# A hybrid decoder layer on one core: the first weight units, the bias rows, the block turns and the key raws in another order

## The chip, the core and the metric

The kernel runs on one core of a Trainium2 chip. The metric is the device time of one execution in microseconds (us), as the median of several runs. The profile is of one execution: its "span" runs from the first to the last instruction of the program, and the execution's own time is a little longer than its span.

## What is computed

One layer for 256 tokens of width 2048, all in float32: a half-step SwiGLU block, a mixer (8 attention heads of 128 beside a state-space model, joined by one output projection), and a second half-step SwiGLU block.

```python
x = x + 0.5 * swiglu(rms_norm(x, ffn1_norm), gate, up, down)     # 2048 -> 5632 -> 2048
h = rms_norm(x, mix_norm) @ w_in                                 # q | k | v | u, 1024 columns each
attn = mixture_of_dilations(rms_norm(q), rms_norm(k), v, rel_bias)
y = gelu(s5_ssm(u, ...)); y = y * sigmoid(y @ glu_w + glu_b)
x = x + concat(attn, y) @ w_out
x = x + 0.5 * swiglu(rms_norm(x, ffn2_norm), gate2, up2, down2)
```

The three attention patterns share one bias table (32 buckets by 8 heads). The kernel computes them as one softmax, for which `bias_rows` holds, for each distance, the one-hot bucket, a mask and the logarithm of how many patterns see it.

## The kernel before

**Units.** Every large product is a list of passes (`Pass`): 256 tokens (two PSUM accumulators of 128) by 512 output columns, over all blocks of 128 of the contraction. A pass is cut into groups of four such blocks, and a group into two units. A unit is two blocks by two token halves by three matmuls of 128x128 by 128x512: float32 is split into a high and a low float32r part, and high x high (line 336), high x low weight (337) and low activation x high weight (338) are summed. So a unit is 12 matmuls. The first feed-forward block is 264 units, the mixer 104, the second feed-forward block 264.

**One loop, `run`, sets the order** on all engines. A group's weights (1 MB) are loaded on SyncE's (SP's) queue into one of three buffers `raw`; `split` makes of each half the high part `wh` on ScalarE (ACT, line 292) and the low part `wl` on VectorE (DVE, lines 295 and 297), four units ahead at most (`WB`). After each unit's matmuls `step` advances every other piece of work, written as Python generators: one `yield` is one unit of TensorE (PE) time. Since each engine runs its instructions strictly in the order written, these counts fix who stands behind whom. The very first pass pair (gate and up columns 0 of the first block) is the only one whose groups are interleaved; everything later goes pass after pass.

**The start.** x arrives in pieces of 256 and 512 columns; `Normed.feed` turns them with PE transposes (line 194), and `close` makes `xth` and `xtl`, their high and low parts with the gain. Normalising by the row's root mean square comes later, at eviction (`rstd`, finished by small GpSimd (POOL) operations).

**Bias table.** After the first squares, `other_gains` loads small gains on POOL's queue, and four steps later turns them on PE. `bias_table` then loads the bucket table (`rel`) and `bias_rows` (`oh`) on the same queue, and two steps later a PE matmul (line 1146) joins them. Between the two, `ssm_prepare` has begun: it loads its parameters on POOL's queue, turns b on PE (line 500), and for four pieces of 16 groups forms powers on DVE (676 to 678), which PE multiplies (708).

**Turns by blocks.** `by_blocks` transposes 32x32 blocks on DVE into one tile `blocks` (139), stores it to DRAM (142) and reads it back with rows and blocks exchanged (145), so that PE has no part in it. Each feed-forward column group uses it for its hidden values (in `up_done`); so do the residual's blocks 0 to 2 when they feed the next stage (`feed_by_blocks`). Residual block 3, which is ready last, is turned by PE (`feed`). Column groups 5 and later wait for the state-space preparation, whose space they reuse.

**Mixer.** Passes come in the order u0, u1, k0, q0, k1, q1, v0, v1. The tile `qk` has two halves. `qk_done` writes the raw projection of a pass to the first half, q's turned copy goes to the second. `k_prepare` takes squares on ACT, an inverse root on DVE (lines 113 to 121), scales on ACT (894) and turns on PE (880); `q_scale` turns its scales on PE (906); `head` scores four heads of each half (926 to 956). Beside them DVE runs the state-space scan, step after step (795 to 797).

Of the kernel before, what the change touches and what calls it, by code (L numbers as in the profile page):

```python
# [16 lines left out]
P = 128  # L17
# [21 lines left out]
class Pass:  # L39
    def __init__(self, w, n, stat, ks, done=None, delay=0, pre=None, box=None, opens=True, bank="acc"):  # L40
        self.w, self.n, self.stat, self.ks, self.done = w, n, stat, list(ks), done
        self.delay, self.pre, self.opens, self.bank = delay, pre, opens, bank
        self.box = {} if box is None else box


@with_exitstack
def hybrid_layer_kernel(
# [209 lines left out]
    def run(passes, extra, start):  # L257
        g, u = passes[:2]
        groups = [(g, 0), (u, 0), (g, 4), (u, 4), (g, 8), (g, 12), (u, 8), (u, 12)]
        for p in passes[2:]:  # L260
            for k0 in p.ks:
                groups.append((p, k0))
# [4 lines left out]

        def dma():
# [3 lines left out]
            src = p.w[k0 * P:(k0 + 4) * P, p.n * 512:(p.n + 1) * 512].rearrange("(k p) n -> p k n", p=P)  # L272
            if i == 0:
                for k in range(2):
                    sync.dma_start(out=r[:, k:k + 1], in_=src[:, k:k + 1])
                extra(0)
                sync.dma_start(out=r[:, 2:4], in_=src[:, 2:4])
            else:
                sync.dma_start(out=r, in_=src)
            raws[i] = r  # L280
            st["dma"] += 1
            extra(i + 1)

        def split():
            u = st["split"]
            i, s = divmod(u, 2)
# [16 lines left out]
        def ahead(u):  # L303
            while st["dma"] < ng and st["dma"] < st["split"] // 2 + RAWB:
                dma()
            if st["split"] == 0:
                start()
            while st["split"] < 2 * ng and st["split"] <= (u + WB - 1 if u else 0):
                split()
                if st["split"] == 1:  # L310
                    start()
                while st["dma"] < ng and st["dma"] < st["split"] // 2 + RAWB:
                    dma()

        for i, (p, k0) in enumerate(groups):
            if k0 == p.ks[0]:
# [6 lines left out]
            for s in range(2):  # L323
                u = 2 * i + s
                ahead(u)
                h, l = wts.pop(u)
                order = [(kk, t) for kk in range(2) for t in range(NT)]
                if s == 1 and k0 == p.ks[-1]:
                    order = [(kk, t) for t in range(NT) for kk in range(2)]
                for kk, t in order:  # L330
                    k = k0 + 2 * s + kk
                    sh, sl = p.stat(k)
                    first = p.opens and k == p.ks[0]
                    last = p.done is not None and k == p.ks[-1] + 3
                    c = slice(t * P, (t + 1) * P)
                    pe.matmul(acc[t], sh[:, c], h[:, kk, :], start=first, stop=False)  # L336
                    pe.matmul(acc[t], sh[:, c], l[:, kk, :], start=False, stop=False)  # L337
                    pe.matmul(acc[t], sl[:, c], h[:, kk, :], start=False, stop=last)  # L338
                if s == 1 and k0 == p.ks[-1] and p.done:
                    spawn(call(p.done, acc), p.delay)  # L340
                step()


    def ffn(norm, w_gate, w_up, w_down, done, first):
# [31 lines left out]
        def up_done(c):  # L376
            def f(acc):
# [31 lines left out]
    def residual(norm, factor):  # L409
        def done(n):  # L410
            def f(acc):
# [3 lines left out]
                spawn(norm.feed(n) if n == 3 else norm.feed_by_blocks(n))  # L415
# [12 lines left out]
    def ssm_prepare():  # L428
# [237 lines left out]
        for pc in range(4):  # L666
# [218 lines left out]
    def k_prepare(raw, dst):  # L885
# [9 lines left out]
        yield 2  # L895
        yield from flipped(raw, dst, ident, 1.0)

    def q_scale(n, raw):
# [5 lines left out]
        yield 2  # L904
# [5 lines left out]
    def q_flip(n, raw, dst):  # L910
        while mx["scored"] < 4 * n:
            yield
        yield from flipped(raw, dst, flip, qkg)

    def head(h):
# [3 lines left out]
        qt = mx["qk"][:, 1024:2048].rearrange("p (h s) -> p h s", h=4)[:, i, :]  # L919
# [67 lines left out]
    def mixer(norm, out_done):  # L987
# [20 lines left out]
        def qk_done(which, n):  # L1008
            def f(acc):
                assert not any(alive(mx[x]) for x in ("prep_k0", "prep_k1", "rq0", "qT0") if x in mx)  # L1010
                raw = mx["qk"][:, 0:1024].rearrange("p (t x) -> p t x", t=NT)
# [4 lines left out]
                else:  # L1016
                    dst = mx["qk"][:, 1024:2048].rearrange("p (h s) -> p h s", h=4)
# [58 lines left out]
        for n in range(2):  # L1076
            ps.append(Pass(w_in[0], 6 + n, norm.stat, ks, u_done(n)))
# [18 lines left out]
    with tc.manual_schedule():  # L1096
# [18 lines left out]
        def other_gains():  # L1115
# [3 lines left out]
            pool.dma_start(out=grow[49:50], in_=k_norm)  # L1119
            pool.memset(flip, 0.0)  # L1120
# [13 lines left out]
            yield  # L1134
            yield from bias_table()

        def bias_table():
            rel = small([34, NH], "rel")
            pool.memset(rel, 1.0)
            pool.dma_start(out=rel[0:32], in_=rel_bias)  # L1140
            oh = slots.tile([34, SPAN], F32, name="oh", tag="s1a")
            pool.dma_start(out=oh, in_=bias_rows)
            yield
            yield
# [106 lines left out]
```

## Time and profile before

| | us |
|---|---|
| median of 3 runs | 1803.52 |
| lowest, highest run | 1800.95, 1804.94 |
| profiled execution, its own time | 1803.12 |
| its span | 1801.2 |
| PE busy | 1786.6 (99%) |
| DVE busy | 1058.7 (59%) |
| ACT busy | 845.0 (47%) |

Times in the profile are counted from the span's start. A row of the timeline gives start, duration, engine, line, operation, what it writes and reads, and in brackets how long the engine was idle ahead of it and what ended that. Matmuls overlap, so a matmul of 0.39 us is followed by the next about 0.23 us later; PE's busy share says that something was under way, not that it ran at full rate. The granted clock is the share of full speed that PE was given.

### The profile page before, as it was taken

The numbers are of one execution on the slowest core, as the hardware profiler recorded it, in microseconds if no ns is written. First come the engines' busy times: TensorE is split into PE (matmuls) and PEld (weight loads), VectorE is DVE, ScalarE is ACT, GpSimd is POOL, SyncE is SP. The second block draws the span as 40 slices with busy tenths as digits, with TensorE's granted clock in tenths as the row PEclk, the third lists the DMA queues.
The fourth block names the chain that finished last, engine by engine and source line by source line (L and its number), as shares of the span: only waits on it lengthen the run. The fifth ranks groups of instructions, "written<-read, shape, count | busy, mean of one in ns | idle before, by whom it ended". The sixth has DMA issues, their size and how long they took to land.

```text
span 1801.2 us, 21490 instructions
## 1 busy us (share of the span) xinstructions
PE 1786.6 (99%) x8399; PEld 1475.0 (82%) x8399; DVE 1058.7 (59%) x1368; ACT 845.0 (47%) x1087; POOL 79.3 (4%) x151
## 2 busy tenths in 40 slices
PE   9999999999999999999999999999999999999998
PEld 7788888788888888888788888888888888888887
DVE  5688888455555455544985665555555555544443
ACT  5454444444444444447666555444444444443332
POOL 0400222100000000010000001000000000000000
PEclk9999999999999999999999999999999999999999
DMA  7867988877766676598576585777777677766652
GB/s 257 236 209 228 290 287 281 249 234 220 218 218 206 205 221 221 195 315 284 158 261 203 187 255 190 218 223 212 212 223 219 210 214 222 222 208 210 210 198 105
DMA packets 211013, 402.21 MB, mean 223 GB/s; under 512 B 9581, under 2 KB 40902, under 8 KB 209249
## 3 DMA queue, kind: packets, MB, share of 16 engines
q1 hardware_dynamic: 202672, 378.57, 65.9%
q0 software_dynamic: 6416, 19.13, 3.7%
q10 hardware_dynamic: 1824, 3.15, 0.6%
q8 instruction: 65, 1.06, 0.2%
q14 instruction: 36, 0.29, 0.0%
HBM read 370.00 MB, written 33.44 MB: 224 GB/s over the span
## 4 chain that ended last, share of the span: by engine, by line
PE 93%; DVE 4%; DMA 1%; POOL 1%; ACT 1%; issue 1%; SPq 0%; POOLq 0%; DVEq 0%; ACTq 0%
PE acc L336 30%; PE acc L338 30%; PE acc L337 30%; DVE wl L297 1%; DVE s1a L795 1%; DMA oh<-in_bias_rows_dram 0%; DVE s1a L796 0%; PE tp L336 0%; PE tp L338 0%; PE tp L337 0%; DMA h_d<-blocks 0%; ACT wh L292 0%; DVE slot L797 0%; PE tp L194 0%; PE tp L1108 0%
## 5 line engine op out<-in xcount | busy, mean ns | idle before, releaser
L297 DVE TENSOR_TENSOR wl<-raw,wh 128x1024 fp32r<-128x1024 f32 x628 | 768.6, 1226 | 682.3 <-ACT wh L292 681.9
L292 ACT ACTIVATE wh<-raw 128x1024 fp32r<-128x1024 f32 (+1 forms) x636 | 672.2, 1058 | 882.6 <-PE acc L338 859.3
L336 PE MATMUL acc<-wh,xth 128*128 128x512 f32 x1664 | 655.0, 394 | 1.4 <-ACT wh L292 1.4
L337 PE MATMUL acc<-wl,xth 128*128 128x512 f32 x1664 | 649.1, 390 | 2.7 <-DVE wl L297 2.2
L338 PE MATMUL acc<-wh,xtl 128*128 128x512 f32 x1664 | 649.2, 390 | 0.0
L337 PEld LDWEIGHTS acc<-wl,xth 128*128 128x128 f32 x1664 | 313.4, 188 | 67.5 <-DVE wl L297 2.7
L336 PEld LDWEIGHTS acc<-wh,xth 128*128 128x128 f32 x1664 | 313.2, 188 | 67.0 <-ACT wh L292 1.7
L338 PEld LDWEIGHTS acc<-wh,xtl 128*128 128x128 f32 x1664 | 313.0, 188 | 65.7
L336 PE MATMUL acc<-wh,hid 128*128 128x512 f32 x704 | 273.9, 389 | 0.0
L337 PE MATMUL acc<-wl,hid 128*128 128x512 f32 x704 | 273.9, 389 | 0.0
L338 PE MATMUL acc<-wh,hid 128*128 128x512 f32 x704 | 273.9, 389 | 0.0
L338 PEld LDWEIGHTS acc<-wh,hid 128*128 128x128 f32 x704 | 132.1, 188 | 27.5
L337 PEld LDWEIGHTS acc<-wl,hid 128*128 128x128 f32 x704 | 132.1, 188 | 27.5
L336 PEld LDWEIGHTS acc<-wh,hid 128*128 128x128 f32 x704 | 132.1, 188 | 27.4
L123 POOL TENSOR_TENSOR rs_t<-rstd 128x2 f32<-128x2 f32 x9 | 5.7, 630 | 637.9 <-DVE rstd L115 637.5
L139 DVE STREAM_TRANSPOSE blocks<-sil 128x512 f32<-128x512 f32 x44 | 28.6, 687 | 7.6 <-DMA h_d<-blocks 7.6
L424 POOL DMA_DIRECT2D out_dram<-res x6 | 3.3, 552 | 645.2 <-DVE res L422 645.1
L380 DVE SCALAR_TENSOR_TENSOR sil<-acc,rstd,sil 128x512 f32<-128x512 f32 x44 | 30.7, 740 | 0.0
L130 DVE TENSOR_TENSOR hid<-sil,hid 128x512 fp32r<-128x512 f32 x44 | 28.3, 684 | 0.0
L369 ACT ACTIVATE sil<-acc,rstd 128x512 f32<-128x512 f32 x44 | 27.5, 675 | 0.0
L129 ACT ACTIVATE hid<-sil 128x512 fp32r<-128x512 f32 x44 | 25.0, 614 | 0.0
L657 POOL DMA_DIRECT2D t_d<-k_d x32 | 18.0, 580 | 24.5 <-DMA k_d<-slot 24.2
(324 smaller groups left out, 848.7 us busy)
## 6 DMA issues: line engine op xcount, KB each, us to landing
raw<-in_ffn_w_up_dram SPq DMA_DIRECT2D x88, 1024.0 KB, 5.9
raw<-in_ffn_w_down_dram SPq DMA_DIRECT2D x88, 1024.0 KB, 5.1
raw<-in_ffn_w_gate_dram SPq DMA_DIRECT2D x87, 1024.0 KB, 5.8
raw<-in_w_in_dram SPq DMA_DIRECT2D x32, 1024.0 KB, 5.6
raw<-in_w_out_dram SPq DMA_DIRECT2D x16, 1024.0 KB, 6.0
h_d<-blocks SPq DMA_DIRECT2D x28, 512.0 KB, 7.0
sil<-h_d SPq DMA_DIRECT2D x88, 128.0 KB, 7.1
m_d<-s4b POOLq DMA_DIRECT2D x16, 256.0 KB, 4.9
```

The source lines that it names most:

```text
L129: act.activation(out=h, in_=src, func=AF.Copy)
L130: vec.tensor_tensor(out=l, in0=src, in1=h.bitcast(F32), op=ALU.subtract)
L139: vec.transpose(out=b[:, :, t].rearrange("p j (k c) -> p j k c", k=4), in_=src[:, t, :].rearrange("p (k j c) -> p j k c", k=4, j=4))
L292: act.activation(out=h[:, c], in_=src[:, c], func=AF.Copy)
L297: vec.tensor_tensor(out=l, in0=src, in1=h.bitcast(F32), op=ALU.subtract)
L336: pe.matmul(acc[t], sh[:, c], h[:, kk, :], start=first, stop=False)
L337: pe.matmul(acc[t], sh[:, c], l[:, kk, :], start=False, stop=False)
L338: pe.matmul(acc[t], sl[:, c], h[:, kk, :], start=False, stop=last)
L369: act.activation(out=sil[c][:, t, :], in_=acc[t], func=AF.Silu, scale=norm.scale(t))
L380: vec.scalar_tensor_tensor(out=a[:, t, :], in0=acc[t], scalar=norm.scale(t), in1=a[:, t, :], op0=ALU.mult, op1=ALU.mult)
L657: pool.dma_start(out=stores[0][1], in_=stores[0][2])
L795: vec.tensor_tensor(out=tm, in0=a8, in1=prev.unsqueeze(1).broadcast_to([P, 2, 2, NG]), op=ALU.mult)
```

## The change

Five edits, all of order; the arithmetic stays the same but for where a transpose is made.

1. **First units.** The first two groups (gate and up) are loaded in halves, and their units run as gate first half, up first half, gate second half, up second half. In the first unit the four high x high matmuls come first, then the low activations, then the low weights.
2. **Shared first passes.** A pass may be marked `shared`: it and the next are then interleaved as the first two of the program always were. u0 with u1 and the second feed-forward block's gate with up column 0 are marked too.
3. **Bias rows.** `rel` and `oh` are loaded right after the small gains, ahead of the state-space parameters, and their matmul comes one step earlier.
4. **Turns.** Residual block 3 is turned by `feed_by_blocks` like the others. A hidden turn waits until the one of the column group before has ended. The preparation has one step fewer per piece (behind its last powers).
5. **Keys.** k0 and q1 keep their raw projection in the second half of `qk`, and q's copy goes to the other half; scaled keys and q's inverse roots are used one step later (`yield 3`), and `q_flip` waits for its key to be prepared, no longer for four scored heads.

```diff
+        self.shared = shared
...
-        g, u = passes[:2]
-        groups = [(g, 0), (u, 0), (g, 4), (u, 4), (g, 8), (g, 12), (u, 8), (u, 12)]
-        for p in passes[2:]:
-            for k0 in p.ks:
-                groups.append((p, k0))
+        groups = []
+        passes = list(passes)
+        while passes:
+            p = passes.pop(0)
+            if p.shared:
+                q = passes.pop(0)
+                groups += [(p, 0), (q, 0), (p, 4), (q, 4), (p, 8), (p, 12), (q, 8), (q, 12)]
+            else:
+                groups += [(p, k0) for k0 in p.ks]
...
+        units = [(0, 0), (1, 0), (0, 1), (1, 1)] + [(i, s) for i in range(2, ng) for s in range(2)]
...
+            if i == 0:
+                rs = [rawp.tile([P, 4, 512], F32, name=nm("raw"), tag="raw") for _ in range(2)]
+                for v, a, b in ((0, 0, 1), (0, 1, 2), (1, 0, 2), (0, 2, 4), (1, 2, 4)):
+                    sync.dma_start(out=rs[v][:, a:b], in_=part(*groups[v])[:, a:b])
+                    if v == 1 and a == 0:
+                        extra(0)
...
+            order = [(kk, t, v) for kk in range(2) for t in range(NT) for v in range(3)]
+            if u == 0:
+                order = [(kk, t, v) for v in (0, 2, 1) for kk in range(2) for t in range(NT)]
...
-                    while c >= 5 and first and alive(mx["pre"]):
+                    while (c >= 5 and first and alive(mx["pre"])) or (c and alive(turn[c - 1])):
                         yield
...
-                           (lambda: finish(mx["pre"])) if c == 7 and first else None))
+                           (lambda: finish(mx["pre"])) if c == 7 and first else None, shared=c == 0))
...
-                spawn(norm.feed(n) if n == 3 else norm.feed_by_blocks(n))
+                spawn(norm.feed_by_blocks(n))
...
             for k in range(1, 9, 2):
                 powers(wk[:, :, k:k + 2, :], k, 2, cs, csw)
                 yield from beat()
-                if k != 3:
+                if k in (1, 5):
                     yield from beat()
...
-        yield 2
+        yield 3
         yield from flipped(raw, dst, ident, 1.0)
...
         rsqrt_(rs, ss, 8, 1.0 / HD)
-        yield 2
+        yield 3
         ps = tps()
         pe.matmul(ps[:, 0:8], flip, rs, start=True, stop=True)
...
-        while mx["scored"] < 4 * n:
+        while alive(mx[f"prep_k{n}"]):
             yield
...
-                raw = mx["qk"][:, 0:1024].rearrange("p (t x) -> p t x", t=NT)
+                o = 1024 if (which == "k") == (n == 0) else 0
+                raw = mx["qk"][:, o:o + 1024].rearrange("p (t x) -> p t x", t=NT)
...
-            ps.append(Pass(w_in[0], 6 + n, norm.stat, ks, u_done(n)))
+            ps.append(Pass(w_in[0], 6 + n, norm.stat, ks, u_done(n), shared=n == 0))
...
             pool.dma_start(out=grow[48:49], in_=q_norm)
             pool.dma_start(out=grow[49:50], in_=k_norm)
+            rel = small([34, NH], "rel")
+            pool.memset(rel, 1.0)
+            pool.dma_start(out=rel[0:32], in_=rel_bias)
+            oh = slots.tile([34, SPAN], F32, name="oh", tag="s1a")
+            pool.dma_start(out=oh, in_=bias_rows)
             pool.memset(flip, 0.0)
...
-            yield
-            yield from bias_table()
...
+            yield 2
             ps = tps()
             pe.matmul(ps[:NH, 0:SPAN], rel, oh, start=True, stop=True)
```

How the edits move instructions at three places, as the built programs list them (line, operation, what it writes and reads, shape; line numbers of the change's rows are the changed file's).

SP's queue at the start of the program: `res` is x, `raw_144` the gate's first group, `raw` of `up_dram` the up's. Before:

```order
L1100 DMA res_83<-in_x_dram 128x2x256
L275 DMA raw_144<-in_ffn_w_gate_dram 128x512 x2
L1184 DMA res_83<-in_x_dram 128x2x256
L277 DMA raw_144<-in_ffn_w_gate_dram 128x2x512
L279 DMA raw_149<-in_ffn_w_up_dram 128x4x512
L1187 DMA res_84<-in_x_dram 128x2x512
```

And now:

```order
L1117 DMA res_83<-in_x_dram 128x2x256
L288 DMA raw_144<-in_ffn_w_gate_dram 128x512 x2
L288 DMA raw_145<-in_ffn_w_up_dram 128x2x512
L1196 DMA res_83<-in_x_dram 128x2x256
L288 DMA raw_144<-in_ffn_w_gate_dram 128x2x512
L288 DMA raw_145<-in_ffn_w_up_dram 128x2x512
L1199 DMA res_84<-in_x_dram 128x2x512
```

The up's first half has come ahead of x's second 256 columns; the bytes up to x's next piece are the same.

DVE behind the state-space preparation, where the hidden turns of column groups 5 and 6 (`sil` to `blocks`) follow among the low weights. Before:

```order
L297 TENSOR_TENSOR wl_2838<-raw_2744,wh_2837 128x1024
L380 SCALAR_TENSOR_TENSOR sil_555<-acc_2684,rstd_137,sil_555 128x512
L380 SCALAR_TENSOR_TENSOR sil_555<-acc_2685,rstd_137,sil_555 128x512
L139 STREAM_TRANSPOSE blocks_2862<-sil_555 128x4x128 x2
L297 TENSOR_TENSOR wl_2868<-raw_2744,wh_2867 128x1024
L139 STREAM_TRANSPOSE blocks_2887<-sil_555 128x4x128 x2
L297 TENSOR_TENSOR wl_2891<-raw_2785,wh_2890 128x1024
```

And now, from the turn of group 5 up to that of group 6:

```order
L140 STREAM_TRANSPOSE blocks_2845<-sil_561 128x4x128 x2
L314 TENSOR_TENSOR wl_2849<-raw_2754,wh_2848 128x1024
L314 TENSOR_TENSOR wl_2868<-raw_2754,wh_2867 128x1024
L314 TENSOR_TENSOR wl_2886<-raw_2792,wh_2885 128x1024
L396 SCALAR_TENSOR_TENSOR sil_561<-acc_2710,rstd_137,sil_561 128x512
L396 SCALAR_TENSOR_TENSOR sil_561<-acc_2711,rstd_137,sil_561 128x512
L314 TENSOR_TENSOR wl_2908<-raw_2792,wh_2907 128x1024
L314 TENSOR_TENSOR wl_2926<-raw_2830,wh_2925 128x1024
L314 TENSOR_TENSOR wl_2942<-raw_2830,wh_2941 128x1024
L314 TENSOR_TENSOR wl_2960<-raw_2871,wh_2959 128x1024
L314 TENSOR_TENSOR wl_2976<-raw_2871,wh_2975 128x1024
L314 TENSOR_TENSOR wl_2994<-raw_2911,wh_2993 128x1024
```

One low weight stood between the two turns; now nine stand there (the last fence ends with the ninth), and group 6's turn follows those.

DVE in the mixer, where the inverse root of k1 (`qk_rs`) begins. Before, from the row behind the scan to that root's first rows:

```order
L947 RECIPROCAL stat<-stat 128x2
L948 SCALAR_TENSOR_TENSOR stat<-stat 128x2
L949 SCALAR_TENSOR_TENSOR stat<-stat 128x2
L113 TENSOR_SCALAR rs_ms_1018_6791<-qk_ss_6717 128x8
L114 TENSOR_SCALAR rs_i_6793<-rs_ms_1018_6791 128x8
L115 TENSOR_SCALAR qk_rs_6718<-rs_i_6793 128x8
```

And now:

```order
L963 RECIPROCAL stat<-stat 128x2
L964 SCALAR_TENSOR_TENSOR stat<-stat 128x2
L965 SCALAR_TENSOR_TENSOR stat<-stat 128x2
L950 SCALAR_TENSOR_TENSOR s5a_5910<-tp_6746,rq,s5b_5911 128x128
L952 SCALAR_TENSOR_TENSOR s5a_5910<-tp_6746,rq,s5b_5911 128x256
L956 TENSOR_REDUCE stat<-s5a_5910 128x1
L957 TENSOR_REDUCE stat<-s5a_5910 128x1
L958 TENSOR_SCALAR stat<-stat 128x2
L114 TENSOR_SCALAR rs_ms_1017_6787<-qk_ss_6706 128x8
```

The heads have slid one unit back, so that the fourth head's logits now stand in the same unit as k1's inverse root, ahead of it; the root itself has kept its unit, and PE's turn of k1 comes one unit later.

More of the change, by code (lines that the diff above doesn't have):

```diff
@@ L39, with __init__ @@
 class Pass:
-    def __init__(self, w, n, stat, ks, done=None, delay=0, pre=None, box=None, opens=True, bank="acc"):
+    def __init__(self, w, n, stat, ks, done=None, delay=0, pre=None, box=None, opens=True, bank="acc", shared=False):
         self.w, self.n, self.stat, self.ks, self.done = w, n, stat, list(ks), done
@@ L266, in run, with part, spent @@
         st = {"dma": 0, "split": 0}
+        units = [(0, 0), (1, 0), (0, 1), (1, 1)] + [(i, s) for i in range(2, ng) for s in range(2)]
+        def part(p, k0):
+            return p.w[k0 * P:(k0 + 4) * P, p.n * 512:(p.n + 1) * 512].rearrange("(k p) n -> p k n", p=P)
+        def spent():
+            n = st["split"]
+            return n // 2 if n >= 4 else max(0, n - 2)
         def dma():
@@ L270, in dma @@
             p, k0 = groups[i]
-            r = rawp.tile([P, 4, 512], F32, name=nm("raw"), tag="raw")
[L272 to L279, printed above, removed]
+            if i == 0:
[4 more added lines that the diff above has]
+                        extra(0)
+                raws[0], raws[1] = rs
+                st["dma"] = 2
+                extra(2)
+                return
+            r = rawp.tile([P, 4, 512], F32, name=nm("raw"), tag="raw")
+            sync.dma_start(out=r, in_=part(p, k0))
             raws[i] = r
@@ L303, in ahead @@
         def ahead(u):
-            while st["dma"] < ng and st["dma"] < st["split"] // 2 + RAWB:
+            while st["dma"] < ng and st["dma"] < spent() + RAWB:
                 dma()
@@ L307, in ahead @@
                 start()
[L308 removed]
+            while st["split"] < 2 * ng and st["split"] <= (u + WB - 1 if u else 1):
                 split()
@@ L311, in ahead @@
                     start()
-                while st["dma"] < ng and st["dma"] < st["split"] // 2 + RAWB:
+                while st["dma"] < ng and st["dma"] < spent() + RAWB:
                     dma()
-        for i, (p, k0) in enumerate(groups):
-            if k0 == p.ks[0]:
+        for u, (i, half) in enumerate(units):
+            p, k0 = groups[i]
+            if k0 == p.ks[0] and half == 0:
                 if p.pre:
@@ L322, in run @@
             acc = p.box["acc"]
[L323 to L341, printed above, removed]
+            ahead(u)
+            h, l = wts.pop(u)
+            end = half == 1 and k0 == p.ks[-1]
+            order = [(kk, t, v) for kk in range(2) for t in range(NT) for v in range(3)]
+            if u == 0:
+                order = [(kk, t, v) for v in (0, 2, 1) for kk in range(2) for t in range(NT)]
+            elif end:
+                order = [(kk, t, v) for t in range(NT) for kk in range(2) for v in range(3)]
+            for kk, t, v in order:
+                k = k0 + 2 * half + kk
+                sh, sl = p.stat(k)
+                first = p.opens and k == p.ks[0] and v == 0
+                last = p.done is not None and k == p.ks[-1] + 3 and v == 2
+                pe.matmul(acc[t], (sh, sh, sl)[v][:, t * P:(t + 1) * P], (h, l, h)[v][:, kk, :], start=first, stop=last)
+            if end and p.done:
+                spawn(call(p.done, acc), p.delay)
+            step()
     def ffn(norm, w_gate, w_up, w_down, done, first):
```

16 lines of the change are left out of this document (4 added, 12 removed).

## The prediction, made before the change was run

> **What bounds the kernel now.** I read the page's engine shares first, then PE's waits, then the clock and the idle time in windows around each wait, and last the timelines there.
>
> ```profile
> span 1801.2 us, 21490 instructions
> PE 1786.6 (99%) x8399; PEld 1475.0 (82%) x8399; DVE 1058.7 (59%) x1368; ACT 845.0 (47%) x1087; POOL 79.3 (4%) x151
> ```
>
> PE is the bound over the whole program. 1801.2 less 1786.6 leaves 14.6 us in which it does nothing, and a change of order can gain only from these, from full-rate work that ran at a lower clock, and from PE work that is dropped. The undisturbed rate is this:
>
> ```profile
> 149.68 0.39 PE L337 MATMUL acc<-wl,xth 128*128 128x512 f32 x1
> 149.90 0.39 PE L338 MATMUL acc<-wh,xtl 128*128 128x512 f32 x1
> ```
>
> One matmul each 0.227 us (twelve from 149.68 on take 2.72), so a unit is 2.72 us and 632 units are 1719 us that no edit touches. PE's waits, with total, count and longest:
>
> ```profile
> PE tp L1146 <- DMA oh<-in_bias_rows_dram: 2.3, 1, 2.3
> PE acc L337 <- DVE wl L297: 2.2, 1, 2.2
> PE acc L336 <- ACT wh L292: 1.4, 1, 1.4
> PE tp L880 <- ACT s4a L894: 1.1, 2, 0.8
> PE tp L880 <- ACT s5a L958: 0.6, 1, 0.6
> PE acc L337 <- DVE wl L295: 0.5, 1, 0.5
> PE tp L906 <- DVE qk_rs L121: 0.4, 1, 0.4
> ```
>
> They sum to 8.5 us. Each lies at one of the edits. Two of them carry a second price, which the windows show (PE, PEld, DVE, ACT, POOL busy, granted clock, DMA share, GB/s):
>
> ```profile
> 10.52:13.93 3.41, 1.47 (x8) 0.84 (x7) 1.88 (x4) 2.75 (x6) 0.00 (x0) 1.00 1.04 386
> 13.93:17.34 3.41, 3.41 (x10) 2.64 (x9) 2.77 (x6) 2.26 (x4) 0.00 (x0) 0.50 0.69 194
> 75.37:78.78 3.41, 3.41 (x10) 2.71 (x9) 3.34 (x8) 1.07 (x1) 1.56 (x3) 0.50 0.83 275
> 348.40:351.80 3.40, 3.04 (x13) 2.54 (x14) 3.40 (x4) 0.21 (x1) 0.00 (x0) 1.00 0.65 188
> ```
>
> Behind the wait at the start and behind that for the bias rows, PE's clock is 0.50 for one stretch of 3.41 us: half of it, 1.7 us, is lost each time. The stretch behind the third stop, that for `wl` at about 346 to 348, has 1.00.
>
> **First units: 3.65 us.** The second unit waits twice, 1.4 for `wh` and then 0.5 for `wl`; the last row is the landing of the issue above it:
>
> ```profile
> 10.55 0.60 PE L194 MATMUL tp<-ident,res 128*128 128x128 f32 x4
> 12.59 0.49 PE L336 MATMUL acc<-wh,xth 128*128 128x512 f32 x1 [1.45 <-ACT wh L292]
> 11.18 0.84 ACT L175 ACTIVATE xth<-tp,gain_f 128x256 fp32r<-128x256 f32 x2 [3.80 <-PE tp L194]
> 2.71 0.47 SPq L277 DMA_DIRECT2D raw<-in_ffn_w_gate_dram  x1
> DMA to landing us min/median/max: 6.6/6.6/6.6
> ```
>
> It needs x's second piece turned, evicted and its weights split, in that order on ACT. Now the up's first half stands between, which needs only the first piece. The gate's second half landed at 2.71 + 6.6, about 9.4; at 386 GB/s, with the new order's 1.3 MB ahead of its end, the up's first half should land at about 8.6 (estimate). Split by ACT and DVE it is there at about 10.5, when PE ends the first unit and the four turns (10.55 + 0.4). So the second unit starts at about 10.9 and the third at 13.6, with x's second piece evicted by 12.9 and its first low weight split by 13.5. Gain: 1.45 + 0.50 + 1.7 for the half-clock stretch = 3.65. Bounds: nothing to 3.65. Near the top, since every landing keeps 0.1 us or more.
>
> **Bias rows: 4.0 us.**
>
> ```profile
> 64.61 0.56 POOL L1142 DMA_DIRECT2D oh<-in_bias_rows_dram  x1
> oh<-in_bias_rows_dram POOLq DMA_DIRECT2D x1, 51.0 KB, 8.9
> s2b<-in_ssm_b_im_dram POOLq DMA_DIRECT2D x1, 256.0 KB, 8.6
> 56.30 0.53 POOL L447 DMA_DIRECT2D s2b<-in_ssm_b_im_dram  x1
> 67.27 1.09 PE L500 MATMUL tp<-ident,s2b 64*128 64x64 f32 x8
> ```
>
> The small gains end ahead of the parameters' loads, of which b's imaginary part stands at 56.3, so `oh` is issued by 55 instead of at 64.6 and lands, with 8.9, by 64; PE asks for it one unit before the 71.4 at which it stopped, at about 68. The wait of 2.3 and its half-clock stretch of 1.7 go: 4.0. What is moved past pays: three instructions of about 0.5 us each (the memset and two issues) now stand ahead of the parameters on POOL, so b's imaginary part is issued at about 57.7 and lands, with 8.6, at 66.3. PE turns it at 67.27, and 1 us is left. If it is late, PE waits at line 500 instead.
>
> **Turns: 2.2 us.**
>
> ```profile
> 346.30 1.30 DVE L139 STREAM_TRANSPOSE blocks<-sil 128x512 f32<-128x512 f32 x2 [7.60 <-DMA h_d<-blocks]
> ```
>
> Two hidden turns stand one low weight apart, the second needs the buffer that the first is still storing, and DVE stands 7.6 us with the low weights behind it. With the second turn started when the first has ended (nine low weights later, 24 us), the store is done. The turned values are read by the down passes alone, which follow the last of eleven column groups. So the 2.2 us go with nothing in their place. Of the rest of this edit, the preparation's step:
>
> ```profile
> 223.80 0.69 DVE L678 TENSOR_TENSOR slot<-slot,tp 128x512 f32<-128x512 f32 x1
> ```
>
> PE multiplies these powers now one unit after they are begun, not two. This one ends at 224.5, and PE's next unit starts at 225.5: 1 us to spare. In the three later pieces DVE also has hidden turns, and the margin is nearer 0. I charge 0.3 us; bounds 0 and 1.2 (a turn pair of 1.3 us wholly in the way, once).
>
> **Residual block 3 and shared passes: 1.8 us.**
>
> ```profile
> 756.67 0.60 PE L194 MATMUL tp<-ident,res 128*128 128x128 f32 x4
> 757.03 0.48 PE L336 MATMUL acc<-wh,xth 128*128 128x512 f32 x1
> ```
>
> Four PE transposes take 0.44 us of matmul time (0.36 to the next start and 0.08 lost on it). Block 3 of two stages is 16 transposes, four such groups: 4 x 0.44 = 1.76 us. In exchange the block travels (the two rows of landings are those of the block stores and of the loads of `turn`, from their issue):
>
> ```profile
> DMA to landing us min/median/max: 2.9/7.0/8.7
> DMA to landing us min/median/max: 3.5/6.9/8.3
> L175 ACT ACTIVATE xth<-turn,gain_mx x12: 491/494/512, 595.0 to 716.4; 128x256 fp32r<-128x256 f32 x12
> L178 DVE SCALAR_TENSOR_TENSOR xtl<-turn,gain_mx,xth x24: 343/347/352, 595.9 to 717.6; 128x128 fp32r<-128x128 f32 x24
> 765.00:775.00 10.00, 10.00 (x46) 8.29 (x45) 4.27 (x4) 4.56 (x5) 5.32 (x14) 1.00 0.97 350
> ```
>
> Counted from the start of the stage's first unit: the sum with the residual and two block transposes among low weights, 4 us (estimate); store 7.0; loads 6.9, done at 18 to 20; two ACT and four DVE instructions, 2.4 us, behind the weights' splits: 24 at the latest. Because the first two passes are interleaved, ten units stand ahead of block 3's first, 27.2 us. Without sharing it would be at unit 6, 16.3. Margin: 3 us; if both transfers take their longest (8.7 and 8.3), nothing. The ten units are the cover; bounds 1.76 and, with 3 us late in both stages, -4.2.
>
> **Keys: 1.3 us.**
>
> ```profile
> 860.00:921.00 61.00, 58.93 (x278) 48.17 (x277) 57.43 (x159) 41.64 (x98) 2.15 (x4) 1.00 0.51 160
> 885.32 0.35 DVE L934 SCALAR_TENSOR_TENSOR s5a<-tp,rq,s5b 128x128 f32<-128x128 f32 x1
> 886.69 1.22 DVE L297 TENSOR_TENSOR wl<-raw,wh 128x1024 fp32r<-128x1024 f32 x1
> 889.28 0.17 DVE L113 TENSOR_SCALAR rs_ms<-qk_ss 128x8 f32<-128x8 f32 x1
> 891.59 1.22 DVE L297 TENSOR_TENSOR wl<-raw,wh 128x1024 fp32r<-128x1024 f32 x1
> 891.46 0.49 PE L956 MATMUL tp<-flip,s5a 128*128 128x128 f32 x3
> ```
>
> PE's four waits (1.1 + 0.6 + 0.4 us) are all of the 2.07 that it is idle here, and each stop also costs the overlap of two matmuls (0.39 alone against 0.227): 2.1 + 4 x 0.16 = 2.7. One more step takes each of them away. But DVE is busy 57.43 of 61, and now the fourth head's logits (885.32 to 886.69 here, 1.4 us) stand with the root (889.28 to 891.59, 2.3 us) ahead of one low weight. That weight ended at 892.81 before, and the same rows stand ahead of it now; PE, no longer held, asks for it at about 891.7. So PE gets a new wait of about 1.0 and some 0.4 behind it: 2.7 - 1.4 = 1.3. Bounds 0 and 2.7.
>
> **Sum.** 3.65 + 4.0 + 2.2 - 0.3 + 1.76 + 1.3 = 12.6 us. The profiled execution took 1803.1 (span 1801.2 and 1.9 around it); the median of the runs shown is 0.4 higher. 1803.1 - 12.6 = **1790.5 us**.
>
> [...] The row first: stops of 1.9 and 2.3 us were each followed by a stretch at 0.50, one of 2.2 was not. [...]
>
> **The rivals.**
>
> 1. *DVE takes over as the bound* between 860 and 921 and in the preparation: every wait of the keys comes back at the low weights, and the preparation pays its 1.2. For it: 94% busy. Against: only one weight there is late. 12.6 - 1.3 - 0.9 = 10.4, 1792.7. Chance 0.15.
> 2. *b comes late.* The parameters' loads slip by more than 1 us, and PE stops at line 500 as it did at 1146: about 1.2 us, with a half-clock stretch of 1.7 behind: 12.6 - 2.9 = 9.7, 1793.4. For it: margin of 1 us among landings of 8.6. Chance 0.10.
> 3. *The half-clock stretches come anyway*, at another place: 12.6 - 3.4 = 9.2, 1793.9. For it: a stop of 2.2 us had none. Against: both begin right behind a stop. Chance 0.06.
> 4. *The first units don't do what they should:* 512 KB of up's weights ahead of x's second piece make that piece late instead, and the third unit waits as the second did: 12.6 - 3.65 = 8.95, 1794.2. For it: the DMA share is 1.04 there. Chance 0.08.
> 5. *Slower: block 3 arrives after its unit, in both stages.* One mechanism: its store and loads queue with 1 MB weight loads and the state-space model's own. Each microsecond that the block lands after 23 us from the stage's start (27.2 less the 4 from landing to ready) is one of PE's idle. To undo 12.6, both stages must be 4.6 us late with a half-clock stretch of 1.7 behind each. With 3 us more for each transfer than its longest they are 6 us late: 2 x (6 + 1.7) = 15.4, 1805.9. For it: the DMA share is 0.97 from 765 to 775, when the loads would land. Against: the transfers' longest are 8.7 and 8.3 among such loads. Chance 0.03.
>
> The forecast itself has 0.58.
>
> **How the numbers follow.** The forecast's own bounds are 1787 (keys in full 2.7, no charge for the preparation, a little overlap at each removed stop) and 1793. Rivals 1 to 4 end by 1794.2, with 1 or 2 us for two of them together: the range is 1787 to 1796, which leaves out the slower rival and the pairs. About 0.2% (3.6 us) is what this kernel's runs can tell, which spread over 4 us. All cases but the fifth gain more than 8 us: faster 0.94, no change 0.03 (block 3 late in one stage only, with a rival beside it), slower 0.03.
>
> **What would show it.** In the changed profile no wait for `oh` and none at line 500; no stretch at 0.50 up to 80 us; no wait of DVE for `h_d`; 32 transposes of `res` on PE, and no wait for block 3's `xth` at unit 10 of either later stage; between 885 and 897 (some 10 us earlier by then) no wait for scaled keys but one of about 1 us for a low weight. PE's idle time should fall from 14.6 to some 7 us. I would be wrong if a stretch at 0.50 stands behind a new stop, or if PE waits for `wl` in many units of the mixer.

## The result, and the profile after

The changed kernel takes 1789.34 us (median; 1789.09 to 1789.56) against 1803.26 us before (1800.95 to 1804.94): the ratio is 0.9924, interval 0.9906 to 0.9941. That is 13.9 us less, where 12.6 were forecast; 1789.3 lies 1.2 us below the forecast of 1790.5 and inside the range. The profiled execution took 1789.56 us.

The head of the page after, and PE's waits:

```profile
span 1787.8 us, 21499 instructions
PE 1780.3 (100%) x8383; PEld 1469.8 (82%) x8383; DVE 1061.2 (59%) x1380; ACT 845.2 (47%) x1087; POOL 80.1 (4%) x151
```

```profile
PE tp L1125 <- POOL ident masks.py:199: 1.4, 1, 1.4
PE acc L354 <- DVE wl L314: 0.6, 1, 0.6
PE acc L354 <- DVE xtl L179: 0.4, 1, 0.4
PE tp L972 <- ACT s5a L967: 0.3, 1, 0.3
PE tp L195 <- DMA res<-in_x_dram: 0.3, 1, 0.3
```

PE's idle time has fallen from 14.6 to 1787.8 - 1780.3 = 7.5 us. All seven waits quoted in the prediction are gone. The wait of 1.4 us for `ident`, at the program's start, was there before too; four short ones, 1.6 us together, have come. Two of these, for x (0.4 and 0.3), are missing in a second trace of the changed kernel, that of the control run below, so they come and go between executions. Of the signs that the prediction named, one did not come: DVE still waits once for a block store (2.1 us, up to 1026; the same wait stood in the kernel before), and PE does not wait there.

Where the time went can be read off both traces by the start of the same unit's first matmul (unit numbers run through the program from 0; a number stands for the same work in both, except in the first four units and in the first sixteen of each later stage, from 264 and from 368 on, where the order is new but the units are as large):

| place | unit | before | after | difference | gained in between |
|---|---|---|---|---|---|
| behind the first units | 5 | 26.88 | 23.09 | -3.79 | 3.8 |
| behind the bias rows | 21 | 79.84 | 72.11 | -7.73 | 3.9 |
| behind the preparation | 107 | 321.66 | 313.93 | -7.73 | 0.0 |
| behind the hidden turns | 117 | 351.39 | 341.13 | -10.26 | 2.5 |
| behind the mixer's block 3 | 268 | 763.07 | 751.85 | -11.22 | 1.0 |
| behind the keys | 328 | 962.87 | 950.58 | -12.29 | 1.1 |
| behind the last block 3 | 372 | 1089.15 | 1075.91 | -13.24 | 1.0 |
| end of the span | | 1801.19 | 1787.76 | -13.43 | 0.2 |

Against the terms of the prediction (3.65, 4.0, -0.3, 2.2, 1.76, 1.3) no line is off by more than 0.35 us in this pair of executions. Part of that is luck. The second trace of the kernel before against that of the control gains 2.6, 3.8, 0.0, 4.2, 1.0, 1.1 and 1.0 at the same places: the total is near (13.9, against 13.4 of the table), but the first units bring 1 us less than forecast and the hidden turns 2 us more. Whether each line has the cause that was given for it is another question, and for two of them it hasn't.

### The profile page after: what moved, and what is told of

Same layout as the page of the kernel before. It is cut to its first block, busy times and chain, and to the rows that moved or that the text cites. A ratio compares the mean times of both kernels' runs of the same rounds, so it can differ in the third digit from the quotient of the medians.

```text
span 1787.8 us, 21499 instructions
## 1 busy us (share of the span) xinstructions
PE 1780.3 (100%) x8383; PEld 1469.8 (82%) x8383; DVE 1061.2 (59%) x1380; ACT 845.2 (47%) x1087; POOL 80.1 (4%) x151
## 4 chain that ended last, share of the span: by engine, by line
PE 96%; DVE 2%; ACT 1%; DMA 1%; issue 0%; SPq 0%; ACTq 0%
PE acc L354 92%; PE tp L354 1%; DMA raw<-in_ffn_w_gate_dram 1%; DVE wl L314 1%; DVE s1a L811 0%; ACT wh L309 0%; PE tp L822 0%; DVE s1a L812 0%; PE tp L724 0%; PE tp L787 0%; ACT tp L886 0%; PE tp L997 0%; PE tp L825 0%; DVE slot L813 0%; PE tp L896 0%
## 5 line engine op out<-in xcount | busy, mean ns | idle before, releaser
L354 PE MATMUL acc<-wh,hid 128*128 128x512 f32 x1408 | 433.7, 389 | 0.0
L354 PE MATMUL acc<-wh,s4b 128*128 128x512 f32 x64 | 20.8, 394 | 0.0
L354 PE MATMUL acc<-wh,s2a 128*128 128x512 f32 x64 | 20.8, 393 | 0.0
L354 PE MATMUL acc<-wh,slot 128*128 128x512 f32 x64 | 20.7, 393 | 0.0
```

The costliest lines, as they stand in the source:

```text
L354: pe.matmul(acc[t], (sh, sh, sl)[v][:, t * P:(t + 1) * P], (h, l, h)[v][:, kk, :], start=first, stop=last)
```

## The experiments

Each kernel is the changed one with one thing altered, unless it says otherwise. It is compared with the changed kernel's control run below (1789.24, 1789.01 to 1789.62). The three sets ran on three chips, on which the kernel before had medians of 1802.7, 1803.1 and 1803.6; the control belongs to the third, so differences of less than half a microsecond are not read.

**The changed kernel again, as control.**

> The changed kernel once more, as control for the three beside it: 1789.3, all executions within 1 us, since no stop is left that fills enough of a clock window for a stretch at 0.50.

Measured: 1789.24 us. Nine executions of the changed kernel, over both measurements, lie between 1789.01 and 1789.62; thirteen of the kernel before, timed beside the first experiments, lie between 1800.94 and 1804.74. Not only the time but the spread has gone, and the next runs show from where.

**First units as before.**

```diff
-        units = [(0, 0), (1, 0), (0, 1), (1, 1)] + [(i, s) for i in range(2, ng) for s in range(2)]
...
+            i, s = divmod(u, 2)
...
+            if i == 0:
+                for k in range(2):
+                    sync.dma_start(out=r[:, k:k + 1], in_=src[:, k:k + 1])
+                extra(0)
+                sync.dma_start(out=r[:, 2:4], in_=src[:, 2:4])
+            else:
+                sync.dma_start(out=r, in_=src)
```

> The changed kernel (1789.3 us) with its first units as before: the first two groups loaded whole behind x's second piece, units gate, gate, up, up; the shared passes stay. My theory, that the second unit's stop (1.45 + 0.5 us) and the half-clock stretch behind it (1.7) were the cost: 1793.0, with both stops and a stretch at 0.50 in the profile. Rival (the stretch does not hang on the stop): about 1791.2, the stop without the stretch. Rival (the start gained only because the clock rose 2 us earlier in the one profile of the change, 5.1 against 7.1 us): 1789.3 to 1790.2 whenever it rises early.

Measured: 1791.83 us median; three executions between 1791.71 and 1791.84 and one of 1793.20. So 2.6 us come back, not 3.65, and the 1793.0 of my theory was missed. PE's waits and the two windows of 3.41 us around the stop (columns as in the prediction's windows):

```profile
PE acc L341 <- ACT wh L297: 1.4, 1, 1.4
PE acc L342 <- DVE wl L300: 0.8, 2, 0.5
```

```profile
9.60:13.01 3.41, 1.96 (x10) 1.25 (x8) 0.93 (x3) 1.81 (x5) 0.00 (x0) 1.00 1.05 397
13.01:16.42 3.41, 2.92 (x13) 2.32 (x13) 3.41 (x6) 2.78 (x6) 0.00 (x0) 1.00 0.67 186
```

The same stop as in the kernel before, and no half-clock stretch behind it. The stop is worth 2.6 us; the stretch that the prediction's trace has behind it (3.41 us at 0.50, so 1.7 us) is no part of that. Whether one came on top in the execution of 1793.20 is not shown, since that one was not traced.

**Bias rows as before.**

```diff
-            rel = small([34, NH], "rel")
-            pool.memset(rel, 1.0)
-            pool.dma_start(out=rel[0:32], in_=rel_bias)
-            oh = slots.tile([34, SPAN], F32, name="oh", tag="s1a")
-            pool.dma_start(out=oh, in_=bias_rows)
             pool.memset(flip, 0.0)
...
-            yield 2
+            yield
+            yield from bias_table()
```

> The changed kernel with the bias rows loaded behind the state-space parameters and joined one step later, as before. My theory: PE stops about 2.3 us for them and runs the next stretch of 3.4 us at 0.50: 1793.3. Rival, that stretch and stop are independent: 1791.6 with the stop alone.

Measured: 1793.23 us (1792.37 to 1794.57), 4.0 more than the control. In its trace the stop and the stretch are both back (the wait, and the windows):

```profile
PE tp L1163 <- DMA oh<-in_bias_rows_dram: 2.1, 1, 2.1
```

```profile
66.82:70.24 3.42, 1.35 (x8) 0.69 (x8) 3.18 (x11) 1.06 (x1) 0.00 (x0) 1.00 0.56 146
70.24:73.65 3.41, 3.41 (x12) 2.71 (x12) 3.34 (x8) 1.06 (x1) 1.56 (x3) 0.50 0.78 287
```

This execution is the fastest of the four, 3.1 us above the control; what the slower ones have on top was not traced.

**The kernel before, a second trace.**

> The kernel before once more, for a second trace of it. My theory: the same two stretches at 0.50, behind the stops at about 12 and 71 us, about 1803. Rival, that they depend on where the clock's own windows fall, which moves from one execution to the next: one of them is missing or elsewhere, and the time is 1.7 us shorter for each that is missing.

Measured: 1803.45 us, from 1800.49 to 1806.35 over ten executions. Its windows around the three stops, each pair being the window with the stop and the one behind it:

```profile
9.17:12.58 3.41, 1.96 (x12) 1.44 (x10) 0.57 (x2) 1.45 (x4) 0.00 (x0) 1.00 1.05 403
12.58:15.99 3.41, 2.91 (x12) 2.16 (x13) 3.41 (x7) 2.51 (x5) 0.00 (x0) 1.00 0.70 211
70.61:74.02 3.41, 2.10 (x12) 1.38 (x13) 3.17 (x11) 0.45 (x2) 0.00 (x0) 1.00 0.50 139
74.02:77.43 3.41, 3.41 (x10) 2.64 (x9) 3.34 (x8) 0.81 (x1) 1.56 (x3) 0.50 0.82 250
343.67:347.09 3.42, 1.14 (x6) 0.60 (x4) 2.37 (x4) 1.06 (x1) 0.00 (x0) 1.00 0.06 22
347.09:350.50 3.41, 3.32 (x8) 2.64 (x9) 3.41 (x4) 0.00 (x0) 0.00 (x0) 0.50 0.74 192
```

The prediction's trace had stretches behind the first stop and the second; this one has them behind the second and the third. The stops are the same. What differs is when the granted clock changes. In the prediction's trace it does so, after the first 10 us, at 13.93, 17.34, 75.37, 78.78 and 1799.10: these lie 1, 17, 1 and 504 steps of 3.413 us apart. In this trace the two stretches begin at 74.02 and 347.09, 80 such steps apart (273.07 / 3.413 = 80.0). From 13.93 to 74.02 it is 17.6 steps, so the two grids lie differently, and one stop of about 2 us falls into one step in one execution and over two in the other. The first stop stands at the same time in both traces (1.45 us idle up to 12.59 and up to 12.54, then 0.50 more), but here the boundary at 12.58 (18 steps ahead of 74.02) divides it, while in the prediction's trace all of it lies ahead of the boundary at 13.93. At the third stop, 2.3 of 2.4 us lie in one window here. In the prediction's trace 1.9 of 2.2 us do, and no stretch followed. These are that trace's windows with the second stop, which brought a stretch, and with the third, which did not (on the grid, unlike the prediction's 348.40:351.80):

```profile
71.96:75.37 3.41, 1.70 (x10) 1.07 (x10) 3.17 (x10) 0.48 (x1) 0.00 (x0) 1.00 0.58 141
345.02:348.43 3.41, 1.51 (x7) 0.93 (x5) 2.13 (x3) 1.06 (x1) 0.00 (x0) 1.00 0.13 45
```

The third rival, that the stretches come anyway, falls with these runs: between the first 10 us and the program's end none was seen without a stop in the window ahead, and the first trace of the changed kernel, in which PE waits at most 0.6 us at a time there, has 1.00 from 5.1 to 1786.8 us. But my own theory, one stretch for each of the first two stops, falls too: there are three candidates, and in each of the two traces two of them were followed by a stretch.

The spans of all 45 executions of the kernel before that were timed beside these experiments say how often. They lie in three groups with nothing between: 12 from 1798.5 to 1799.6, 21 from 1800.8 to 1801.7 and 12 from 1802.2 to 1802.7. Both traces, with two stretches each, belong to the middle one (1801.2). The steps of about 1.7 to 2 us fit one, two and three stretches, two on average; the outer groups were not traced, so that is a reading and not shown. It is not all of the spread either: the time outside the span varies from 1.9 to 3.9 us in these executions, against 1.7 to 1.8 in the nine of the changed kernel, and why is open.

In these two traces stops of 1.9 to 2.4 us were followed by half clock at four places, the windows ahead having 1.14 to 2.10 us of PE work, and at two they were not. Busy time alone doesn't order the windows (1.51 and 1.96 stayed at full clock; 1.70 and 2.10, both with the small bias matmul, did not), and what exactly is counted stays open.

**Without the rule on hidden turns.**

```diff
-                    while (c >= 5 and first and alive(mx["pre"])) or (c and alive(turn[c - 1])):
+                    while c >= 5 and first and alive(mx["pre"]):
                         yield
```

> The changed kernel without the rule that a hidden turn waits for the one of the column group before. My theory: DVE stands some 7 us for the block store near 339 us and PE 2.2 us for a low weight behind it, 2.5 with the overlap lost: 1791.8. Rival, that the shorter preparation has already moved the two turns apart: 1789.3.

Measured: 1788.78 us (1788.33 to 1789.32). Nothing comes back, and the rival holds. DVE's block transposes of groups 5 and 6 in this kernel, and between them the row that makes group 6's values:

```profile
323.70 1.30 DVE L140 STREAM_TRANSPOSE blocks<-sil 128x512 f32<-128x512 f32 x2
331.86 1.40 DVE L396 SCALAR_TENSOR_TENSOR sil<-acc,rstd,sil 128x512 f32<-128x512 f32 x2
337.30 1.30 DVE L140 STREAM_TRANSPOSE blocks<-sil 128x512 f32<-128x512 f32 x2
```

In the kernel before the turns were begun at 336.30 and, after 7.6 us of waiting, at 346.30. Of the 12.6 us by which group 5's turn is earlier here, 8.6 are the lead that this kernel has by then anyway (unit 107 starts at 313.10 against 321.66). The other 4 come from the shorter preparation, which ends four units, 10.9 us, earlier, and why that moves the turns apart can be read from the program. Group 7's first pass begins by running whatever is left of the preparation (`finish`), and each step of that advances all other work too. As the programs are built, three steps are run there in one place with the longer preparation, so that group 6's values and group 5's turn come together, and group 6's turn one low weight later. With the shorter one nothing is left to run: group 5's turn stands ahead of group 6's values, and group 6's turn begins 13.6 us after group 5's, by which time the store is done.

**The longer preparation, with the rule; and both undone.**

```diff
             for k in range(1, 9, 2):
                 powers(wk[:, :, k:k + 2, :], k, 2, cs, csw)
                 yield from beat()
-                if k in (1, 5):
+                if k != 3:
                     yield from beat()
```

> The changed kernel with the longer preparation (one step more per piece), the rule on hidden turns kept. Since taking that rule alone away changed nothing, either of the two must have cleared the stop at 339 us. If either suffices: 1789.3, no stop. If the shorter preparation alone did it: 1791.8 and PE's stop of 2.2 us. If the shorter preparation also cost what I charged it: 0.3 less than either.

Measured: 1788.85 us (1788.42 to 1789.10). For the second kernel the rule on turns is taken out as above as well.

> Both undone, the longer preparation and no rule on turns. If either suffices: the stop is back, 1789.3 + 2.5 = 1791.8, and up to 1793.5 in executions where a half-clock stretch follows it. If neither is the cause: 1789.3.

Measured: 1793.59 us (1790.88 to 1795.21). DVE's wait for the block store (two waits in all, the longest 8.7 us) and PE's for the low weight behind it are back, with a stretch:

```profile
DVE blocks L140 <- DMA h_d<-blocks: 10.9, 2, 8.7
PE acc L354 <- DVE wl L314: 3.9, 2, 3.3
```

```profile
338.73:342.14 3.41, 0.55 (x2) 0.48 (x3) 3.01 (x4) 0.41 (x1) 0.00 (x0) 1.00 0.22 77
342.14:345.55 3.41, 3.41 (x9) 2.67 (x8) 2.80 (x3) 0.00 (x0) 0.00 (x0) 0.50 0.68 181
```

So either half of the edit clears the stop and only both undone bring it back, at 4.4 us in the median. That is a little more than the 2.5 to 4.2 expected; PE's wait of 3.3 is longer here than the 2.2 and 2.4 in the kernel before. The four executions lie 4.3 us apart. A stretch of 1.7 in some of them and not in others is too little for that; what else differs was not traced. The shorter preparation costs nothing that can be told: with it undone the time is 0.4 us lower, and in the traces the difference from the control (0.6 us there) stands already at unit 5, ahead of the preparation. The start moves by about as much between two executions of the changed kernel itself: unit 5 starts 0.5 us sooner in the control's trace than in the first.

**Block 3 turned by PE.**

```diff
-                spawn(norm.feed_by_blocks(n))
+                spawn(norm.feed(n) if n == 3 else norm.feed_by_blocks(n))
```

> The changed kernel with residual block 3 turned by PE again in both stages; the shared passes stay. My theory, that the 16 transposes cost what they hold PE: 1789.3 + 1.8 = 1791.1, half of it at the start of each later stage. Rival, that another wait there takes their place (low weights, with DVE's reads of the block): 1789.3.

Measured: 1791.33 us (1790.97 to 1792.25), 2.1 more. The unit starts move by 0.96 us over the first units of the mixer and by as much over those of the last stage, and PE has no wait there. The transposes cost what they hold PE.

**Block 3 by DVE and DRAM, but no shared passes in the later stages.**

```diff
-            turned = yield from by_blocks(res[n], self.area[:, n % 2])
+            turned = yield from by_blocks(res[n], self.area[:, n % 2], 2 if n == 3 else 3)
...
-                           (lambda: finish(mx["pre"])) if c == 7 and first else None, shared=c == 0))
+                           (lambda: finish(mx["pre"])) if c == 7 and first else None, shared=c == 0 and first))
...
-            ps.append(Pass(w_in[0], 6 + n, norm.stat, ks, u_done(n), shared=n == 0))
+            ps.append(Pass(w_in[0], 6 + n, norm.stat, ks, u_done(n)))
```

> The changed kernel with block 3 by DVE and DRAM, but the first passes of the two later stages not interleaved (the block's high and low parts are issued one step earlier, so that they stand ahead of their unit). My theory, that the ten units ahead are the cover: the block lands 20.4 us after the stage's start and its low part is done at 23, while PE comes to it at 16.3, so PE stops 5 to 7 us in each stage, with a half-clock stretch behind a stop where it fills enough of a clock window: 1789.3 + 10 to 14 + 0 to 3.4, 1799 to 1807. Rival, that the transfers are faster with fewer weights ahead of them: 1789.3 to 1794.

Measured: 1797.43 us (1795.84 to 1800.37 over ten executions), 8.2 more, and less than the 1799 to 1807 that I expected. PE stops for block 3 twice, 4.3 us in the mixer and 1.5 in the last stage; the first leaves a whole window of 3.41 us empty, and the next is at 0.50:

```profile
PE acc L354 <- ACT xth L176: 5.8, 2, 4.3
```

```profile
757.41:760.82 3.41, 0.00 (x0) 0.00 (x0) 0.00 (x0) 0.05 (x1) 0.00 (x0) 1.00 1.06 262
760.82:764.23 3.41, 2.90 (x7) 2.32 (x8) 2.81 (x13) 2.60 (x5) 0.00 (x0) 0.50 1.00 399
1085.09:1088.50 3.41, 1.98 (x10) 1.32 (x8) 1.33 (x2) 0.91 (x3) 0.00 (x0) 1.00 1.09 276
```

The cover is what I said it was, though less is needed than I expected: PE needs the high part first and stops for that alone, and in the last stage the transfers land sooner (block 3's loads after 5.7 to 5.9 us, against 8.7 to 9.3 in the mixer; that the state-space model's loads beside them are the reason there was not shown). Block 3 by DVE saves 2 us of PE and would cost 8 without the shared passes.

**The keys' edit undone whole, and its pauses alone.**

```diff
-        yield 3
+        yield 2
         yield from flipped(raw, dst, ident, 1.0)
...
-        yield 3
+        yield 2
         ps = tps()
         pe.matmul(ps[:, 0:8], flip, rs, start=True, stop=True)
...
-        while alive(mx[f"prep_k{n}"]):
+        while mx["scored"] < 4 * n:
...
-                o = 1024 if (which == "k") == (n == 0) else 0
-                raw = mx["qk"][:, o:o + 1024].rearrange("p (t x) -> p t x", t=NT)
+                raw = mx["qk"][:, 0:1024].rearrange("p (t x) -> p t x", t=NT)
```

The second kernel takes only the first two hunks.

> The changed kernel with the keys' edit undone whole: one half of the tile for all raw projections, two steps where there are three, the rule of four scored heads. My theory: PE's stops at the turns of k1 and at q's inverse roots come back (2.7 us with the overlap lost) and the new one at a low weight (0.6 + 0.3) goes: 1789.3 + 1.1 = 1790.4. Rival, that DVE holds PE there in any case: 1789.3.

> The changed kernel with only the two longer pauses of the keys' edit undone (two steps again); halves and rule kept. If the pauses are what removed PE's stops: like the whole edit undone, 1790.4, PE waiting for scaled keys at the turns and for q's roots. If the halves and the rule (the heads' place) did it: 1789.3.

Measured: 1789.99 us for both (1789.77 to 1790.06, and 1789.69 to 1790.85), 0.75 more, where 1.1 was expected. PE's waits are the same in both traces; those of the whole edit undone:

```profile
PE tp L896 <- ACT s4a L910: 0.8, 1, 0.8
PE tp L896 <- ACT s5a L974: 0.6, 1, 0.6
PE tp L922 <- DVE qk_rs L122: 0.4, 1, 0.4
```

The pauses are the whole of this edit's worth; the halves and the new rule are worth nothing by themselves here. And what the pauses give is what is left after DVE has taken its part, as the prediction had it. In the changed kernel's trace (DVE, then PE):

```profile
876.29 0.35 DVE L950 SCALAR_TENSOR_TENSOR s5a<-tp,rq,s5b 128x128 f32<-128x128 f32 x1
877.66 0.18 DVE L114 TENSOR_SCALAR rs_ms<-qk_ss 128x8 f32<-128x8 f32 x1
880.00 1.22 DVE L314 TENSOR_TENSOR wl<-raw,wh 128x1024 fp32r<-128x1024 f32 x1
881.28 0.50 PE L354 MATMUL acc<-wl,xth 128*128 128x512 f32 x1 [0.63 <-DVE wl L314]
884.34 0.84 PE L972 MATMUL tp<-flip,s5a 128*128 128x128 f32 x3 [0.27 <-ACT s5a L967]
```

Logits at 876.29, the root at 877.66, the low weight only at 880.00, and PE idle for 0.63 until it is there, then 0.27 for ACT.

**An attempt to do better.** k's inverse root one step later, and x's third piece turned one unit earlier.

```diff
         yield from squares(r4, ss)
-        yield
+        yield 2
         rsqrt_(rs, ss, 8, 1.0 / HD)
...
-                spawn(feed_input(), 2)
+                spawn(feed_input(), 1)
```

> The changed kernel with two further moves: a key's inverse root one step later (so that it no longer stands with the fourth head's logits ahead of one low weight), and x's third piece turned one unit earlier at the start. If DVE's pile of 6.3 us between two low weights is the cause of the stop at 880 us, and x's third piece the cause of that near 20 us: both go, 0.9 + 0.4 + 0.5, about 1787.7. If DVE is simply full there: the stop moves on by a unit and 1788.8 is left. If the later root delays the second half's heads beyond their cover: slower than 1789.3.

Measured: 1790.39 us (1789.89 to 1790.69), 1.1 us slower than the control. PE's waits, and two rows of DVE:

```profile
PE acc L354 <- DVE wl L314: 0.6, 1, 0.6
PE tp L195 <- DMA res<-in_x_dram: 0.6, 1, 0.6
PE tp L724 <- DVE slot L694: 0.6, 1, 0.6
PE tp L822 <- DVE slot L813: 0.5, 1, 0.5
```

```profile
877.14 1.23 DVE L314 TENSOR_TENSOR wl<-raw,wh 128x1024 fp32r<-128x1024 f32 x1
883.14 1.22 DVE L314 TENSOR_TENSOR wl<-raw,wh 128x1024 fp32r<-128x1024 f32 x1
```

Root and logits did come apart, but two low weights are still 6.0 us apart (877.14 to 883.14; 6.3 before, from 873.68 to 880.00), with two scan steps and the root between them, and the stop of 0.6 only moved on by a unit: DVE is full there, as the second of the three expectations said, though its number (1788.8) did not come. The time is slower, as in the third, but not where that looked for it: by the starts of the units, 0.7 of the 1.0 us that this trace loses against the control behind unit 5 is lost in the preparation. The early turn waits for x's landing, and it probably brings everything behind it one unit forward against the column groups, so that a product of the preparation (line 724) now waits for its powers; that this is the reason was not shown by a run of its own. Whether the root of k1 alone, or a scan step moved, would help was not tried.

## Why the prediction was right, and where not

*First units.* The mechanism held: the up's first half landed at 9.1 us (8.6 was estimated), ACT split it from 9.08 on, and the second unit began at 10.50. The size was off in two ways: the stop is worth 2.6 us, not the 1.45 + 0.50 that were charged, and the 1.7 for the half-clock stretch was charged as certain. The prediction's trace had that stretch, and against the control's trace this term reads 4.3; the second trace of the kernel before had none, and the term reads 2.6. The 3.8 of the table is lower than 4.3 because the first trace of the changed kernel waits for x (0.4 and 0.3) and the control's doesn't. The first record of the granted clock, at 1.00, stands at 5.1 us in the first trace of the changed kernel and at 7.1 in that of the kernel before; what that alone was worth at unit 5 was not shown (the control's trace starts it 0.5 us sooner than that first one).

*Bias rows.* 4.0 forecast, 4.0 by undoing, 3.9 by the pair of traces (3.8 by the second pair). POOL's and PE's rows after, and the landings:

```profile
50.60 0.54 POOL L1141 DMA_DIRECT2D oh<-in_bias_rows_dram  x1
54.26 0.54 POOL L463 DMA_DIRECT2D s2b<-in_ssm_b_im_dram  x1
64.23 1.09 PE L516 MATMUL tp<-ident,s2b 64*128 64x64 f32 x8
```

```profile
oh<-in_bias_rows_dram POOLq DMA_DIRECT2D x1, 51.0 KB, 2.1
s2b<-in_ssm_b_im_dram POOLq DMA_DIRECT2D x1, 256.0 KB, 5.9
```

`oh` landed 2.1 us from its issue, not 8.9, now that it stands ahead of the parameters' loads. b's imaginary part was there at 60.2, before PE first asks for b at 64.23. The second rival had no place, with 4 us to spare instead of the 1 that was worked out from old positions.

*Turns.* The sum had 2.2; the table has 2.5, and the second pair of traces, where a stretch followed this stop, 4.2. The step that failed is the cause: "with the second turn started when the first has ended" names the rule on turns, and that rule changes nothing here. The shorter preparation, to which 0.3 us was charged, clears the same stop by itself, and what it cost was nil. I took the order's nine low weights between the two turns for the work of the rule without asking what the shorter preparation had already moved: the two turns stood together because three steps of the preparation were run at once ahead of group 7.

*Block 3 and shared passes.* 1.76 forecast, 1.9 by the traces, 2.1 by undoing. The path of the block, in the changed kernel (store, loads, then ACT, and PE's first row of the stage and of its unit 10):

```profile
744.73 0.37 SPq L143 DMA_DIRECT2D h_d<-blocks  x1
750.58 2.26 SPq L146 DMA_DIRECT2D turn<-h_d  x4
761.20 1.71 ACT L176 ACTIVATE xth<-turn,gain_mx 128x256 fp32r<-128x256 f32 x4 [2.65 <-DMA turn<-h_d]
740.97 0.39 PE L354 MATMUL acc<-wh,xth 128*128 128x512 f32 x1
768.17 0.39 PE L354 MATMUL acc<-wh,xth 128*128 128x512 f32 x1
```

The block is there 20.2 us after the stage's start (18 to 20 were forecast, though the loads took 8.8 to 9.6, more than any before), its low part is done at 763.9, 23 us (24), and PE comes at 27.2 us, as worked out. The fifth rival's mechanism is real: without the ten units of cover it cost 8 us.

*Keys.* 1.3 forecast, 1.1 by the traces, 0.75 by undoing. A new wait for one low weight of 1.0 us and 0.4 behind it was forecast; it measures 0.6 idle (0.9 with the overlap) and 0.3 (0.4).

*The sum.* By undoing one edit at a time, 2.6 + 4.0 + 4.4 + 2.1 + 0.75 = 13.85, against 13.9 measured; each of these is known to half a microsecond at best, so that they meet so closely is luck too. The forecast of 12.6 had the stretches at the first two stops (3.4) and none at the third. On average the three stops seem to bring as many, spread over all three (two by the groups of spans above): the total was near because of that, not because each was placed rightly.

## What to carry to other kernels

A stop of PE had two prices in this kernel: its length, and at some stops a stretch of 3.41 us at 0.50 behind it (1.7 us). Each of two traces of the kernel before shows the second behind two of three stops of 1.9 to 2.4 us, and not behind the same two; so charge it as a chance to every such stop, and look whether the spans gather in steps (here of about 1.7 to 2 us; that these are such stretches was not shown). When two edits lie on one path, ask of each alone whether the stop would still be there; and when a wait is removed from an engine that another keeps nearly full, expect to get what the fuller one leaves (here 0.75 us of 2.7, with DVE busy 57.43 of 61 us).

## What the runs showed of the hardware

A stretch at 0.50 began at 13.93 and 75.37 in one trace of the kernel before (18 steps of 3.413 us apart), at 74.02 and 347.09 in the other (80 steps), with the same three stops. The same load of 51 KB took 8.9 us from issue to landing behind the parameters' loads, with the DMA engines busy (share 1.02 from 64.6 to 67 us, 1.05 up to 70), and 2.1 ahead of them (share 0.32 from 50.6 to 52.7). Whether the loads ahead of it on its queue or the busy engines held it was not separated.
